# One pool for raw and split weights, a closer second row tile and later transposes in a two-layer decoder trunk

## The chip, the cores and the metric

The kernel runs on one core of one Trainium2 chip. The metric is device time in microseconds (us) of one execution, the median of several runs; lower is better.

## What is computed

The reference is a causal decoder trunk of two layers on 256 rows (two row tiles of 128) with a model width of 2048, all in float32:

```
for layer in range(2):
    u = rms_norm(h, mix_norm_pre[layer])
    u = even_mixer(u, ...) if layer == 0 else odd_mixer(u, ...)
    h = h + rms_norm(u, mix_norm_post[layer])
    u = swiglu(rms_norm(h, ffn_norm_pre[layer]), w_gate, w_up, w_down)
    h = h + rms_norm(u, ffn_norm_post[layer])
```

The even mixer is stick-breaking attention beside a gated DeltaNet, the odd one block-sparse attention beside dilated attention, each between an input and an output projection. `swiglu(u)` is `(silu(u @ w_gate) * (u @ w_up)) @ w_down` with a hidden width of 5632, which is 11 columns of 512. Nearly all the bytes are weights: each is read once and used for both row tiles.

## The kernel before, in words

**Six phases.** `run` (L477) plans six phases and runs them in order with `run_phase`: even in (120 steps), even out (32), FFN of layer 0 (264), odd in (96), odd out (32), FFN of layer 1 (264). A step is one weight piece of 256 rows by 512 columns, 512 KB (some of 16 steps of even in are narrower). `self.load_until` (L224) loads a piece with one DMA on SP's queue into a raw place, splits it into a high and a low part of reduced precision (`split`, L214: ACT's copy at L217, DVE's subtraction at L218) and so makes `w`, 8 KB a partition. `step` (L253) multiplies one row tile with a piece: 2 blocks times 3 products (high by high, high by low, low by high) of 512 columns, L261 to L263. With both row tiles a plain piece is 12 products.

**Fast pieces.** In the FFN most gate and up columns are a `FastChunk` (L80): 5 plain pieces, then 3 fast ones for both row tiles at once with 7 block products in place of 8, each of 3 matmuls of 256 columns (`fast_step`, L270, L285 to L287). A fast piece is 21 matmuls, needs two places for `w`, and four sums of weight blocks on DVE ahead of the split (`split_sums`, L244, L247 to L249). At the chunk's end ACT and DVE put the result together (L291 to L299).

**Places.** There are 3 raw places (`RAW`, a pool of their own) and 10 for `w` (`WB`). The framework hands out the places of a pool in turn, so the DMA of piece k waits for the split of piece k-3, and the split of piece k waits until TensorE is done with what stood in its place ten places ago. The two row tiles are `LAG` = 4 pieces apart (8 at the ends of a phase, `run_phase`, L319); fast pieces bring them together.

**The FFN's order.** `plan_ffn` (L625) takes the 11 columns in groups (0), (1,2), (3,4), ... (9,10). A group's down chunks (4 chunks of 2 pieces a column) stand behind the next group's first gate chunk. So a run of chunks without down chunks between them is up 1, gate 2, up 2, gate 3 (four chunks of 8 pieces), then 16 down pieces, and so on; the last run is up 9, gate 10, up 10, and behind it the down chunks of (9,10) end the phase. An up chunk ends with `up_chunk` (L664): DVE multiplies (L666), then TensorE transposes the product (L364) and ACT and DVE split it for the down products.

**Order and queues.** A scheduler in the framework orders each engine's instructions ahead of time by the order in which they are written and by modelled times; an engine then runs its own strictly in order. SP's queue carries the weight loads and the stores of x to DRAM (`store_x`, L714); POOL's carries the loads of norm weights (L413), the reload of x (L474) and some multiplications (L704). Small working tiles come from a pool of 44 (`mem`), PSUM banks from pools of 5 and 3; in the FFN 3 banks are lent, so that 2 are left for transposes and 6 for sums. Each down chunk's sum is added to y in `down_chunk` (L684), which in the last group also squares it, reloads x and multiplies by the norm weight; `end_ffn` (L708) then puts the norm and the residual together and, in layer 0, stores x.

Of the kernel before, what the change touches and what calls it, by code (L numbers as in the profile page):

```python
# [44 lines left out]
WB = 10  # L45
LAG = 4
# [6 lines left out]
RAW = 3  # L53
# [4 lines left out]
FFN_GROUPS = ((0,), (1, 2), (3, 4), (5, 6), (7, 8), (9, 10))  # L58
# [84 lines left out]
class Builder:  # L143
    def __init__(self, tc, I, out, pool):
        self.tc, self.nc, self.I, self.out = tc, tc.nc, I, out
        self.const = pool("const", bufs=1)
        self.wpool = pool("w", bufs=WB)
        self.rpool = pool("raw", bufs=RAW)
# [4 lines left out]
        self.mem = Pool(big, "m", NTILES)  # L153
        self.ps = Pool(psb, "p", NPS)
# [69 lines left out]
    def load_until(self, n, end=None):  # L224

        nc = self.nc
        while self.loaded < min(n + WB if end is None else end, len(self.steps)):
            s = self.steps[self.loaded]
            if sum(a.places for a in self.steps[n:self.loaded + 1]) > WB:
                break  # L230
            raw = self.rpool.tile([P, 2048], F32, name="raw", tag="raw")
            w = [self.wpool.tile([P, 2048], F32R, name="w", tag="w") for i in range(s.places)]
            if s.pair is None:
                n_ = s.src.shape[2]
                raw = raw[:, :1024].rearrange("p (k n) -> p k n", k=2)[:, :, :n_]
                s.wh, s.wl = (a.rearrange("p (k n) -> p k n", k=2)[:, :, :n_] for a in (w[0][:, :1024], w[0][:, 1024:]))
                nc.sync.dma_start(out=raw, in_=s.src)
                self.split(s.wh, s.wl, raw)
            else:
                nc.sync.dma_start(out=raw[:, :1024], in_=s.src.rearrange("p k n -> p (k n)"))  # L240
                self.split_sums(raw.rearrange("p (b n) -> p b n", b=8), s, *w)
            self.loaded += 1
# [27 lines left out]
    def fast_step(self, s):  # L270
# [17 lines left out]
        if s.last:  # L288
            za, zb, zu = self.now(self.mem, 3)
            u = zu[:, lo]  # L290
# [5 lines left out]
            self.mem.give(zu)  # L296
# [22 lines left out]
    def run_phase(self, lo, hi, end):  # L319

        n0 = n1 = lo
        while n1 < hi:
            edge = n0 - lo < LAG_EDGE or hi - n0 <= LAG_EDGE - LAG
            lag = LAG_EDGE if edge else max(LAG, LAG_EDGE - (n0 - lo - LAG_EDGE) // 2)
            if n0 < hi and self.steps[n0].pair is not None:
                if n0 == n1:
                    self.fast_step(self.steps[n0])
                    n0 += 1
# [9 lines left out]
            else:  # L338
                self.step(1, self.steps[n1])
                n1 += 1  # L340
# [136 lines left out]
    def run(self):  # L477
# [31 lines left out]
        for i, ((lo, hi), end) in enumerate(zip(bounds, ends)):  # L509
            if i % 3 == 2:  # L510
                for j in range(PS_FFN):
                    self.ps.lend(self.pa)
                if i == 2:
                    self.mem.give(*self.lev)
            self.run_phase(lo, hi, end)
            if i % 3 == 2:
# [108 lines left out]
    def plan_ffn(self, layer):  # L625
        chunks, waiting = [], []
        g, u, d = self.I["ffn_w_gate"], self.I["ffn_w_up"], self.I["ffn_w_down"]
        for q, grp in enumerate(FFN_GROUPS):
            down = []
            for c in range(4):  # L630
                pieces = [(d[layer, c, 2 * f + j], (4 * i + 2 * j, 4 * i + 2 * j + 1))
                          for i, f in enumerate(grp) for j in range(2)]
                done = lambda t, acc, c=c, q=q: self.down_chunk(t, layer, q, c, acc)
                down.append(Chunk(pieces, self.lhs_h, done))
            for i, f in enumerate(grp):
# [4 lines left out]
                if i == 0:  # L640
                    chunks += waiting
                if self.fast("ffn_w_up", f):
                    chunks.append(self.col_chunk(u[layer], f, lambda out, i=i, f=f: self.up_fast(i, f, out), FastChunk))
                else:
                    chunks.append(self.col_chunk(u[layer], f, lambda t, acc, i=i: self.up_chunk(t, i, acc)))
            waiting = down
        chunks += waiting
        self.sg, self.hT = [None, None], [[], []]
# [3 lines left out]
    def lhs_h(self, t, kt):  # L652
        return self.operands(self.hT[t], kt)
# [10 lines left out]
    def up_chunk(self, t, i, acc):  # L664
        u = self.sg[t]
        self.nc.vector.tensor_mul(u, acc, u)  # L666
        self.hT[t].append(self.transposed(u))
        self.mem.give(u)

    def up_fast(self, i, f, out):  # L670
# [4 lines left out]
        for t in range(2):  # L675
            self.up_chunk(t, i, out[t])
            self.mem.give(out[t])

    def free_hT(self, t):
        for pair in self.hT[t]:  # L680
            self.mem.give(*pair)
        self.hT[t] = []

    def down_chunk(self, t, layer, q, c, acc):  # L684
        nc = self.nc
        if c == 3:
            self.free_hT(t)
# [26 lines left out]
    def store_x(self, t):  # L714
        for c in range(4):
            self.nc.sync.dma_start(out=self.xd[t * P:(t + 1) * P, c * 512:(c + 1) * 512], in_=self.x[t][c])
# [131 lines left out]
    def softmax_attn(self, t, g):  # L848
# [5 lines left out]
        if self.mask is None:  # L854
            self.mask = self.now(self.mem).rearrange("p (a b) -> p a b", a=2)
            nc.gpsimd.dma_start(out=self.mask, in_=self.I["amask"])
        mask = self.mask[:, g // 2, 2 * P - nk:]
# [453 lines left out]
```

## Time and profile before

| | |
|---|---|
| median of 3 runs | 2465.85 us (2463.9 to 2470.06) |
| the profiled execution: own time, span | 2476.57 us, 2474.8 us |
| TensorE matmul (PE) busy | 2393.2 us, 97% |
| VectorE (DVE) busy | 1725.7 us, 70% |
| ScalarE (ACT) busy | 1205.3 us, 49% |
| GpSimd (POOL) busy | 201.3 us, 8% |
| mean granted TensorE clock | 0.986 of full speed |
| weight loads on SP's queue | 808, 430.10 MB moved on that queue |

The profiled execution is 10.7 us (0.4%) above the median. PE's busy share counts a matmul from its start to a modelled end, and matmuls overlap; how fast TensorE really goes is read from the starts of matmuls and from their count in a stretch. PEld is the loading of the stationary operand. In the views "A <- B" means that A stood idle until B was done.

### The profile page before, as it was taken

The numbers are of one execution on the slowest core, as the hardware profiler recorded it, in microseconds if no ns is written. First come the engines' busy times: TensorE is split into PE (matmuls) and PEld (weight loads), VectorE is DVE, ScalarE is ACT, GpSimd is POOL, SyncE is SP. The second block draws the span as 40 slices with busy tenths as digits, with TensorE's granted clock in tenths as the row PEclk, the third lists the DMA queues.
The fourth block names the chain that finished last, engine by engine and source line by source line (L and its number), as shares of the span: only waits on it lengthen the run. The fifth ranks groups of instructions, "written<-read, shape, count | busy, mean of one in ns | idle before, by whom it ended". The sixth has DMA issues, their size and how long they took to land.

```text
span 2474.8 us, 32450 instructions
## 1 busy us (share of the span) xinstructions
PE 2393.2 (97%) x12235; PEld 1992.8 (81%) x12235; DVE 1725.7 (70%) x2373; ACT 1205.3 (49%) x1537; POOL 201.3 (8%) x241
## 2 busy tenths in 40 slices
PE   9999998999999999999988999999999999999997
PEld 7878877778888878887876888887888888878885
DVE  6655765667787867777767555556778786877775
ACT  6654563554544444544445444454454444444543
POOL 0340361200000000000020000000000000000012
PEclk9999998999999999999998999999999999999998
DMA  7634444364556565656575555565565566465655
GB/s 228 204 131 150 136 141 161 122 210 157 188 186 206 163 211 171 204 170 205 182 260 191 170 170 175 180 227 192 164 187 188 185 184 208 154 215 176 204 189 186
DMA packets 132669, 453.67 MB, mean 183 GB/s; under 512 B 15568, under 2 KB 20944, under 8 KB 132512
## 3 DMA queue, kind: packets, MB, share of 16 engines
q1 hardware_dynamic: 124160, 430.10, 54.3%
q0 software_dynamic: 6192, 20.22, 2.6%
q8 instruction: 96, 1.57, 0.2%
q10 hardware_dynamic: 2160, 1.27, 0.2%
q14 instruction: 61, 0.50, 0.1%
HBM read 443.11 MB, written 8.42 MB: 182 GB/s over the span
## 4 chain that ended last, share of the span: by engine, by line
PE 28%; DMA 24%; DVE 19%; ACT 6%; issue 4%; ACTq 0%; POOL 0%; DVEq 0%; POOLq 0%
DVE w L218 12%; DMA raw<-in_ffn_w_gate 9%; DMA raw<-in_ffn_w_down 8%; DMA raw<-in_ffn_w_up 7%; ACT w L217 6%; PE acc L263 5%; PE acc L261 5%; PE acc L262 5%; PE p L263 3%; PE p L262 3%; PE p L261 3%; DVE m L299 1%; DVE raw L247 1%; DVE raw L248 1%; DVE raw L249 1%
## 5 line engine op out<-in xcount | busy, mean ns | idle before, releaser
L218 DVE TENSOR_TENSOR w<-raw,w 128x1024 fp32r<-128x1024 f32 (+2 forms) x808 | 1085.7, 1350 | 551.8 <-ACT w L217 548.9
L217 ACT ACTIVATE w<-raw 128x1024 fp32r<-128x1024 f32 (+2 forms) x808 | 928.7, 1153 | 993.3 <-DVE raw L249 231.5
L261 PE MATMUL acc<-w,m 128*128 128x512 f32 (+2 forms) x1622 | 643.2, 397 | 14.6 <-ACT w L217 5.6
L262 PE MATMUL acc<-w,m 128*128 128x512 f32 (+2 forms) x1622 | 640.4, 396 | 4.0 <-DVE w L218 3.9
L263 PE MATMUL acc<-w,m 128*128 128x512 f32 (+2 forms) x1622 | 639.9, 396 | 2.0 <-DVE m L218 1.2
L261 PE MATMUL p<-w,m 128*128 128x512 f32 x1106 | 439.8, 399 | 6.8 <-ACT w L217 5.7
L262 PE MATMUL p<-w,m 128*128 128x512 f32 x1106 | 439.3, 397 | 4.0 <-DVE w L218 3.7
L263 PE MATMUL p<-w,m 128*128 128x512 f32 x1106 | 438.5, 397 | 0.2 <-DVE m L218 0.2
L261 PEld LDWEIGHTS acc<-w,m 128*128 128x128 f32 x1622 | 307.6, 190 | 84.2 <-ACT w L217 7.9
L262 PEld LDWEIGHTS acc<-w,m 128*128 128x128 f32 x1622 | 307.5, 190 | 75.2 <-DVE w L218 9.4
L263 PEld LDWEIGHTS acc<-w,m 128*128 128x128 f32 x1622 | 307.5, 190 | 70.6 <-DVE m L218 1.8
L261 PEld LDWEIGHTS p<-w,m 128*128 128x128 f32 x1106 | 208.5, 189 | 56.4 <-ACT w L217 8.2
L262 PEld LDWEIGHTS p<-w,m 128*128 128x128 f32 x1106 | 208.7, 189 | 55.2 <-DVE w L218 8.2
L263 PEld LDWEIGHTS p<-w,m 128*128 128x128 f32 x1106 | 208.5, 188 | 49.6 <-DVE m L218 0.6
L286 PE MATMUL p<-w,m 128*128 128x256 f32 x480 | 133.3, 278 | 0.4 <-DVE w L218 0.4
L285 PE MATMUL p<-w,m 128*128 128x256 f32 x480 | 133.4, 278 | 0.0
L287 PE MATMUL p<-w,m 128*128 128x256 f32 x480 | 133.1, 277 | 0.0
L247 DVE TENSOR_TENSOR raw<-raw 128x512 f32<-128x512 f32 x126 | 86.9, 690 | 49.9 <-DMA raw<-in_ffn_w_up 32.2
L285 PE MATMUL acc<-w,m 128*128 128x256 f32 x402 | 111.9, 278 | 0.0
L286 PE MATMUL acc<-w,m 128*128 128x256 f32 x402 | 111.3, 277 | 0.0
L287 PE MATMUL acc<-w,m 128*128 128x256 f32 x402 | 111.3, 277 | 0.0
L286 PEld LDWEIGHTS p<-w,m 128*128 128x128 f32 x480 | 90.4, 188 | 1.6 <-DVE w L218 1.0
(266 smaller groups left out, 2022.9 us busy)
## 6 DMA issues: line engine op xcount, KB each, us to landing
raw<-in_ffn_w_gate SPq DMA_DIRECT2D x176, 512.0 KB, 4.2
raw<-in_ffn_w_up SPq DMA_DIRECT2D x176, 512.0 KB, 4.3
raw<-in_ffn_w_down SPq DMA_DIRECT2D x176, 512.0 KB, 4.3
raw<-in_ev_w_in SPq DMA_DIRECT2D x104, 512.0 KB, 3.4
raw<-in_od_w_in SPq DMA_DIRECT2D x96, 512.0 KB, 3.5
raw<-in_ev_w_out SPq DMA_DIRECT2D x32, 512.0 KB, 4.3
raw<-in_od_w_out SPq DMA_DIRECT2D x32, 512.0 KB, 4.2
xd<-m SPq DMA_DIRECT2D x24, 256.0 KB, 4.1
```

The source lines that it names most:

```text
L217: self.nc.scalar.activation(h, src, AF.Copy)
L218: self.nc.vector.tensor_sub(l, src, h.bitcast(F32))
L247: nc.vector.tensor_sub(b[:, 4:6], b[:, 0:1].broadcast_to([P, 2, 256]), b[:, 1:3])
L248: nc.vector.tensor_sub(b[:, 6], b[:, 1], b[:, 5])
L249: nc.vector.tensor_sub(b[:, 7], b[:, 3], b[:, 6])
L261: nc.tensor.matmul(acc, xh, s.wh[:, j], start=(s.first and j == 0), stop=False)
L262: nc.tensor.matmul(acc, xh, s.wl[:, j], start=False, stop=False)
L263: nc.tensor.matmul(acc, xl, s.wh[:, j], start=False, stop=end)
L285: nc.tensor.matmul(acc, xh, s.wh[:, b], start=s.first and i in (0, 2), stop=True, **kw)
L286: nc.tensor.matmul(acc, xh, s.wl[:, b], start=False, stop=True, **kw)
L287: nc.tensor.matmul(acc, xl, s.wh[:, b], start=False, stop=True, **kw)
L299: nc.vector.tensor_add(z, z, acc)
```

## The change

Raw and split weights come from one pool of 13 places, handed out first in, first out. A load takes the first free place for raw data and the next one or two for `w`, and gives the raw place back at once (behind the others); `w` places come back when the second row tile has used them. A load is made only while `spare` + (places of the piece) are free: 3 outside the FFN, 5 in it. In the FFN the second row tile is 1 piece behind instead of 4. The FFN's transposes become a generator that lets 5 calls of `advance` (one a step) pass first. The columns are grouped (0,1), (2,3), ... (8,9), (10); the down chunks of (8,9) stand behind up 10, and those of (10) last. The stores of x go to POOL's queue. Two tiles of `mem` are saved. The diff, cut:

```diff
-RAW = 3
+WPLACES = 13
+SPARE = 3
+SPARE_FFN = 5
+LAG_FFN = 1
+DEFER = 5
-FFN_GROUPS = ((0,), (1, 2), (3, 4), (5, 6), (7, 8), (9, 10))
+FFN_GROUPS = ((0, 1), (2, 3), (4, 5), (6, 7), (8, 9), (10,))
...
-            if sum(a.places for a in self.steps[n:self.loaded + 1]) > WB:
+            if len(self.wp.free) < s.places + self.spare:
                 break
-            raw = self.rpool.tile([P, 2048], F32, name="raw", tag="raw")
-            w = [self.wpool.tile([P, 2048], F32R, name="w", tag="w") for i in range(s.places)]
+            place = raw = self.wp.pop(1)
+            s.w = [self.wp.pop(1) for i in range(s.places)]
+            w = [a.bitcast(F32R) for a in s.w]
...
+            self.wp.give(place)
             self.loaded += 1
...
-            za, zb, zu = self.now(self.mem, 3)
-            u = zu[:, lo]
+            za, zb = self.now(self.mem, 2)
+            u = zb[:, lo]
...
-            edge = n0 - lo < LAG_EDGE or hi - n0 <= LAG_EDGE - LAG
-            lag = LAG_EDGE if edge else max(LAG, LAG_EDGE - (n0 - lo - LAG_EDGE) // 2)
+            edge = n0 - lo < LAG_EDGE or hi - n0 <= LAG_EDGE - self.lag
+            lag = LAG_EDGE if edge else max(self.lag, LAG_EDGE - (n0 - lo - LAG_EDGE) // 2)
...
                 self.step(1, self.steps[n1])
+                self.wp.give(*self.steps[n1].w)
                 n1 += 1
                 self.load_until(n1)
...
                 if i == 2:
                     self.mem.give(*self.lev)
+                else:
+                    self.mem.give(self.mask)
+                self.spare, self.lag = SPARE_FFN, LAG_FFN
             self.run_phase(lo, hi, end)
+            self.spare, self.lag = SPARE, LAG
...
-                if i == 0:
+                if f == grp[0] and f != NFC - 1:
                     chunks += waiting
...
+            if f == NFC - 1:
+                chunks += waiting
             waiting = down
...
     def lhs_h(self, t, kt):
+        while kt // 4 not in self.hT[t]:
+            assert self.advance()
         return self.operands(self.hT[t], kt)
...
+    def up_fast(self, f, out):
...
         for t in range(2):
-            self.up_chunk(t, i, out[t])
+            u = self.sg[t]
+            self.nc.vector.tensor_mul(u, out[t], u)
             self.mem.give(out[t])
+            self.work.append(self.up_transpose(t, f, u))
+
+    def up_transpose(self, t, f, u):
+        for i in range(DEFER):
+            yield
+        o = yield from self.ps.take()
+        self.transpose4(o, v4(u))
+        self.mem.give(u)
+        h, l = yield from self.mem.take(2)
+        self.split(h.bitcast(F32R), l.bitcast(F32R), o)
+        self.ps.give(o)
+        self.hT[t][f] = (h, l)
...
     def store_x(self, t):
         for c in range(4):
-            self.nc.sync.dma_start(out=self.xd[t * P:(t + 1) * P, c * 512:(c + 1) * 512], in_=self.x[t][c])
+            self.nc.gpsimd.dma_start(out=self.xd[t * P:(t + 1) * P, c * 512:(c + 1) * 512], in_=self.x[t][c])
```


## Rows read from the trace of the kernel before

**Rows 1.** Windows, six phases: length, PE busy (x), PEld, DVE, ACT, POOL, clock, DMA.
```profile
9.30:431.50 422.20, 402.01 (x2063) 336.08 (x2064) 275.00 (x548) 226.60 (x403) 123.61 (x116) 0.96 0.50 163
431.50:545.60 114.10, 110.47 (x542) 90.18 (x541) 67.70 (x110) 57.89 (x99) 17.24 (x24) 1.00 0.50 160
548.50:1301.90 753.40, 735.52 (x3855) 615.12 (x3855) 572.07 (x704) 360.58 (x369) 23.18 (x32) 1.00 0.60 192
1311.50:1614.50 303.00, 302.27 (x1429) 247.54 (x1430) 167.60 (x209) 142.49 (x206) 9.73 (x19) 0.99 0.55 176
1614.50:1710.20 95.70, 95.70 (x439) 77.65 (x438) 54.43 (x70) 47.19 (x69) 4.97 (x11) 1.00 0.64 210
1713.30:2465.30 752.00, 737.71 (x3855) 618.11 (x3855) 568.40 (x706) 354.95 (x363) 19.89 (x25) 0.99 0.60 188
```

**Rows 2.** Timeline, TensorE at a run's end: start us, us, engine, line, xcount.
```profile
705.79 0.28 PE L285 MATMUL p<-w,m 128*128 128x256 f32 x1
...
706.82 0.39 PE L261 MATMUL acc<-w,m 128*128 128x512 f32 x1
...
709.61 0.40 PE L261 MATMUL acc<-w,m 128*128 128x512 f32 x1
...
718.03 0.66 PE L364 MATMUL p<-ident,m 128*128 128x128 f32 x4 [1.26 <-DVE m L666]
```

**Rows 3.** The chain that ended last, by line, from the page.
```profile
DVE w L218 12%; DMA raw<-in_ffn_w_gate 9%; DMA raw<-in_ffn_w_down 8%; DMA raw<-in_ffn_w_up 7%; ACT w L217 6%; PE acc L263 5%; PE acc L261 5%; PE acc L262 5%; PE p L263 3%; PE p L262 3%; PE p L261 3%; DVE m L299 1%; DVE raw L247 1%; DVE raw L248 1%; DVE raw L249 1%
```

**Rows 4.** Waits of SP's queue: us in total, times, longest us.
```profile
SPq L237 <- DVE w L218: 1316.9, 544, 27.1
...
SPq L716 <- DVE m L446: 22.0, 24, 6.7
```

**Rows 5.** Instructions by line and shape: xcount | busy us, mean ns | idle before.
```profile
L218 DVE TENSOR_TENSOR w<-raw,w 128x1024 fp32r<-128x1024 f32 x666 | 822.6, 1239 | 532.2 <-ACT w L217 530.0
L217 ACT ACTIVATE w<-raw 128x1024 fp32r<-128x1024 f32 x666 | 705.1, 1061 | 726.0 <-DMA raw<-in_ffn_w_down 203.2 <-PE acc L263 178.6 <-DMA raw<-in_ffn_w_gate 114.4
...
L218 DVE TENSOR_TENSOR w<-raw,w 128x1792 fp32r<-128x1792 f32 x126 | 252.7, 2020 | 18.1 <-ACT w L217 17.4
...
L247 DVE TENSOR_TENSOR raw<-raw 128x512 f32<-128x512 f32 x126 | 86.9, 690 | 49.9 <-DMA raw<-in_ffn_w_up 32.2 <-DMA raw<-in_ffn_w_gate 16.7
...
L299 DVE TENSOR_TENSOR m<-m,p 128x512 f32<-128x512 f32 x49 | 33.4, 681 | 0.0
...
L293 DVE TENSOR_TENSOR m<-m,p 128x256 f32<-128x256 f32 x26 | 10.8, 417 | 0.8
```

**Rows 6.** Waits of TensorE, FFN of layer 0.
```profile
PE acc L261 <- ACT w L217: 5.6, 2, 4.8
PE p L364 <- DVE m L666: 5.5, 4, 2.4
```

**Rows 7.** Waits of TensorE, FFN of layer 1.
```profile
PE p L261 <- ACT w L217: 5.7, 1, 5.7
```

**Rows 8.** Busy time at an FFN's entrance and at both FFNs' last down chunks.
```profile
545.00:552.00 7.00, 4.62 (x25) 3.48 (x24) 7.00 (x11) 6.00 (x10) 0.60 (x2) 0.87 0.55 208
1246.00:1270.00 24.00, 17.24 (x72) 12.68 (x72) 13.99 (x18) 10.56 (x12) 5.25 (x10) 0.93 0.86 313
2403.00:2430.00 27.00, 21.18 (x114) 17.69 (x113) 17.20 (x19) 10.64 (x11) 6.40 (x12) 0.87 0.88 300
```

**Rows 9.** Timeline, POOL's loads at the end of the first FFN.
```profile
1245.38 2.13 POOL L474 DMA_DIRECT2D m<-xd  x4
```

**Rows 10.** The chain that ended last: its piece there (start us, us, what).
```profile
1248.34 7.47 DMA raw<-in_ffn_w_down
```

**Rows 11.** Weight loads of L237, even out: from issue to landing.
```profile
DMA to landing us min/median/max: 3.4/4.3/6.9
```

**Rows 12.** Weight loads of L237, odd in: from issue to landing.
```profile
DMA to landing us min/median/max: 3.3/3.5/7.7
```

**Rows 13.** Weight loads of L237, odd out: from issue to landing.
```profile
DMA to landing us min/median/max: 3.4/4.1/5.7
```

More of the change, by code (lines that the diff above doesn't have):

```diff
@@ L146, in __init__ @@
         self.const = pool("const", bufs=1)
-        self.wpool = pool("w", bufs=WB)
-        self.rpool = pool("raw", bufs=RAW)
+        wpool = pool("w", bufs=1)
         self.tmp = pool("tmp", bufs=1)
@@ L153, in __init__ @@
         self.mem = Pool(big, "m", NTILES)
+        self.wp = Pool(wpool, "w", WPLACES, (P, 2048))
+        self.spare, self.lag = SPARE, LAG
         self.ps = Pool(psb, "p", NPS)
@@ L339, in run_phase @@
                 self.step(1, self.steps[n1])
+                self.wp.give(*self.steps[n1].w)
                 n1 += 1
@@ L514, in run @@
                     self.mem.give(*self.lev)
+                else:
+                    self.mem.give(self.mask)
+                self.spare, self.lag = SPARE_FFN, LAG_FFN
             self.run_phase(lo, hi, end)
+            self.spare, self.lag = SPARE, LAG
             if i % 3 == 2:
@@ L630, in plan_ffn @@
             for c in range(4):
-                pieces = [(d[layer, c, 2 * f + j], (4 * i + 2 * j, 4 * i + 2 * j + 1))
-                          for i, f in enumerate(grp) for j in range(2)]
+                pieces = [(d[layer, c, 2 * f + j], (4 * f + 2 * j, 4 * f + 2 * j + 1)) for f in grp for j in range(2)]
                 done = lambda t, acc, c=c, q=q: self.down_chunk(t, layer, q, c, acc)
                 down.append(Chunk(pieces, self.lhs_h, done))
-            for i, f in enumerate(grp):
+            for f in grp:
                 if self.fast("ffn_w_gate", f):
@@ L639, in plan_ffn @@
                     chunks.append(self.col_chunk(g[layer], f, self.gate_chunk))
-                if i == 0:
+                if f == grp[0] and f != NFC - 1:
                     chunks += waiting
[L642 to L645, printed above, removed]
+                chunks.append(self.col_chunk(u[layer], f, lambda out, f=f: self.up_fast(f, out), FastChunk))
+            if f == NFC - 1:
+                chunks += waiting
             waiting = down
         chunks += waiting
-        self.sg, self.hT = [None, None], [[], []]
+        self.sg, self.hT = [None, None], [{}, {}]
         return chunks
     def lhs_h(self, t, kt):
+        while kt // 4 not in self.hT[t]:
+            assert self.advance()
         return self.operands(self.hT[t], kt)
@@ L662, in gate_fast @@
             self.nc.scalar.activation(a, a, AF.Silu)
[L664 to L670, printed above, removed]
+    def up_fast(self, f, out):
         if f == NFC - 1:
@@ L675, in up_fast, with free_hT @@
         for t in range(2):
-            self.up_chunk(t, i, out[t])
+            u = self.sg[t]
+            self.nc.vector.tensor_mul(u, out[t], u)
             self.mem.give(out[t])
[L679 to L682, printed above, removed]
+            self.work.append(self.up_transpose(t, f, u))
[9 more added lines that the diff above has]
+        self.hT[t][f] = (h, l)
+    def free_hT(self, t, q):
+        for f in FFN_GROUPS[q]:
+            self.mem.give(*self.hT[t].pop(f))
     def down_chunk(self, t, layer, q, c, acc):
@@ L686, in down_chunk @@
         if c == 3:
-            self.free_hT(t)
+            self.free_hT(t, q)
         if q == 0:
@@ L854, in softmax_attn @@
         if self.mask is None:
-            self.mask = self.now(self.mem).rearrange("p (a b) -> p a b", a=2)
-            nc.gpsimd.dma_start(out=self.mask, in_=self.I["amask"])
-        mask = self.mask[:, g // 2, 2 * P - nk:]
+            self.mask = self.now(self.mem)
+            nc.gpsimd.dma_start(out=self.mask.rearrange("p (a b) -> p a b", a=2), in_=self.I["amask"])
+        mask = self.mask.rearrange("p (a b) -> p a b", a=2)[:, g // 2, 2 * P - nk:]
         mix, e_, pT = yield from self.mem.take(3)
```

1 line of the change is left out of this document (removed).

## The prediction

> **What bounds the kernel now.** I read the stretches by phase first. PE is busy nearly throughout, but a matmul's busy time overlaps its neighbour's, so I count starts [rows 1]. On the timeline twelve 512-column products start in 709.61 - 706.82 = 2.79 us, 0.2325 each, and nine of 256 columns in 706.82 - 705.79 = 1.03, 0.1144 each [rows 2]; four transposes show 0.66, partly overlapped, and I take 0.11 each. An FFN has 201 plain pieces (2412 products), 63 fast ones (1323) and 120 transposes, which is the 3855 of its row. Without a stall it takes 2412 x 0.2325 + 1323 x 0.1144 + 120 x 0.11 = 560.8 + 151.4 + 13.2 = 725.4 us. The two took 753.4 and 752.0 [rows 1]: **54.6 us are lost in the FFNs**, and no change of order can win more there.
>
> Then the chain that ended last: it runs through loads of the three FFN weights (24%), DVE's subtraction at L218 (12%) and ACT's copy at L217 (6%), and only then through PE [rows 3]. SP's queue tells why. It waited 1316.9 us in 544 loads for L218 [rows 4]: a load leaves when the split of the piece three before it is done, since there are 3 raw places. The stream of weights is a loop of load, copy, subtract, load, with three pieces in it. PE runs dry where this loop is slower than PE.
>
> Where that is: at the end of each run of four fast chunks, PE waits for L218's parts and for the transposes, which wait for L666 behind late splits on DVE [rows 2, 6]; and at the last down chunks, where PE waited 4.8 us at once in layer 0 and 5.7 in layer 1 for L217 [rows 6, 7]. There POOL's burst (x and norm weights [rows 9]) made a weight load take 7.47 us [rows 10] with no piece in reserve. The stretch 1246 to 1270 holds 72 products where 24 / 0.2325 = 103 fit, so about 7.2 us are lost; 2403 to 2430 holds 63 fast and 51 other products, 7.2 + 11.9 = 19.1 of 27 us, so 7.9 [rows 8]. Phase ends: **15 us**. At an entrance 25 products (12 of them transposes) stand in 7 us, 4.3 us of work, 2.7 lost to the norm chain [rows 8]; two of them 5.5. What is left, 54.6 - 15 - 5.5 = **34 us, lies at the run ends**, eight of four chunks and some shorter, about 4 us each.
>
> **The change part by part.**
>
> *One pool, inside the FFN.* I followed the list of free places by hand, in the order in which they come back. With 5 spare, plain pieces still turn over three raw places, and their w places were used ten pieces earlier, as before. In fast chunks it differs: five of eight loads take a place that PE gave back with the piece eight before, so they no longer wait for a split. Such a load can leave one chunk ahead less its own piece: 5 x 12 x 0.2325 + 3 x 21 x 0.1144 = 21.2, less 2.4, 18.8 us before its use. A fast piece needs a landing of 4.1 to 4.3 [rows 11, 13], sums and subtraction of 0.69 + 2 x 0.42 (L248 and L249, taken like the 256-column L293) + 2.02 = 3.55 [rows 5], and a copy of about 1.06 x 1792 / 1024 = 1.86: some 9.6. The loop that bound is open. What is late next is DVE. For a gate and an up chunk it has 10 x 1.239 + 6 x 3.55 of splits, 8 x 0.42 + 4 x 0.68 of putting together and 4 x 0.68 of products and their splits, 12.4 + 21.3 + 3.4 + 2.7 + 2.7 = 42.5 us [rows 5], against PE's 2 x 21.2 + 8 x 0.11 = 43.3. That is 98%: DVE keeps up only if it hardly idles, so a reserve still shrinks through a run, more slowly. Bounds for the 34 us: 0 and 34. I take 20, nearer the gain, since DVE's idle time before plain subtractions is nearly all waits for L217 [rows 5], which an earlier load shortens.
>
> *Lag 1* changes no count of products; with w places ten pieces back it puts the first use some three pieces further from the split. It is part of those 20. *Deferring the transposes* I cost at nothing: they already stand 718.03 - 706.82 = 11 us behind the chunk's last fast product [rows 2], beyond five half-pieces of 6 x 0.2325 = 1.4 us, 7 us; what covers this is L666's delay, and if DVE is early, five half-pieces are still enough. *Two fewer tiles* likewise.
>
> *Groups.* Eleven columns in six groups either way, so products and additions to y stay. The runs become four of four chunks and a last of five (up 8 to up 10) in each FFN, where there were four of four, one of two and one of three. In return 16 down pieces, 16 x 2.79 = 45 us of PE work, stand between up 10 and the first product that needs its transposes. The burst of POOL's loads stays where the tiles of the norm come free, at up 10. Bounds for the 15 us: 0 (the longer run arrives with as little reserve) and 15; I take 10.
>
> *Stores on POOL.* 24 stores leave SP, where they held the queue for 22.0 us in all [rows 4], but at phase ends where weights were not what PE waited for [rows 8], so 0. On POOL each costs an issue of 0.54 (2.13 for four like it [rows 9]); four stand near the power of the norm chain, at worst 2.1 us at each of six norms, 0 as taken, since that power waits for the last store's x anyway.
> The Trainium skill, SBUF — State Buffer, "Who interferes with whom", says that a DMA issued from GpSimd starves while VectorE holds their shared port in a two-port mode, and advises another queue, which speaks against this edit; its section on the bandwidth-pool intuition has an example of 0.62 us growing to 3.1. By that a store would cost 2.5 us more, an estimate, 10 us at a norm whose power stood behind four of them. POOL's four loads took 2.13 us with DVE at work [rows 9], and show no such starving.
>
> *One pool, outside the FFN.* With 3 spare the same list alternates just **two** raw places, and w places come back eleven pieces later. The loop then takes landing + 1.06 + 1.24 + 0.1 for two pieces. Even out: 4.3 + 2.4 = 6.7, 3.35 a piece, against 114.1 / 32 = 3.57 of PE. Odd in: 3.5 + 2.4 = 5.9, 2.95 against 303.0 / 96 = 3.16. Odd out: 4.1 + 2.4 = 6.5, 3.25 against 95.7 / 32 = 2.99 [rows 1, 5, 11 to 13]. Only odd out falls behind, 32 x 0.26 = 8.3 us, under a reserve of 11 - 4 - 1 = 6 pieces, 19 us. Bounds: 0 if ACT and DVE take each piece at once (no gain, since nothing waited there for weights), and 43, rival 1 below. With a quarter of a microsecond of queueing at each of the two, 0.04 x 96 + 0.51 x 32 = 20 us just exceeds the reserve; I take 2.
> The Trainium skill, DMA: Bandwidth & Descriptors, "Anatomy of one DMA", gives 2.0 us + bytes / 436,000 for a DMA (fitted on GpSimd's queue), 3.2 us for 512 KB. By that the loop would take 5.6, 2.8 a piece, and two places would always do, cost 0. The medians here are 3.5 to 4.3 us, so the measurement decides, and the margin is thin.
>
> *Start.* The first seven loads find fresh places and x's loads no longer stand behind waiting weights; then the narrow pieces of even in run on two places. Gain and loss of up to 5 us each; I take -1.
>
> **Sum:** -20 - 10 + 2 - 1 = -29. Against the profiled execution 2476.57 gives 2447.6; its median stands 10.7 lower, so **2437 us**. If everything came in, 54.6 - 5.5 and 5 at the start, 2412.
>
> **The rivals.**
> *(1) Two raw places bind outside the FFN: slower.* Place: L237's loads in odd in and odd out, then even in. If queueing makes the loop 7.2 us, 3.6 a piece, odd in loses 0.44 x 96 = 42, odd out 0.61 x 32 = 20, together 62 less a reserve of 19, 43; even in, at 422.2 / 120 = 3.52, loses 0.08 x 120 = 10, inside its reserve. Then 2466 - 31 + 43 = **2478**. It decides from about 7.0 us (3.5 a piece: 0.34 x 96 + 0.51 x 32 - 19 = 30), where it eats the whole gain. For: DVE is 55% and ACT 47% busy in odd in [rows 1], so a split often finds the engine taken. Against: the loop's parts sum to 5.9 there. Chance 0.17.
> *(2) DVE is the bound at the run ends.* At 98% it lags as before, the transposes wait as before, and the run of five arrives empty: only the start and a little of the ends are won, under 7 us, about **2462**. For: the sum above. Against: in the FFNs DVE was busy 572.07 of 753.4 us [rows 1] and stood waiting for ACT. Chance 0.14.
> *(3) The run ends are won, the phase ends are not,* since the burst meets a reserve used up by five chunks: 2437 + 10 = **2447**. Chance 0.14.
> The forecast has 0.55.
>
> **How the numbers follow.** A measurement of this kernel tells about 0.3%, 7.4 us. Faster by more: the forecast, rival 3 and the lucky edge of rival 2, 0.71; within: the rest of rival 2 and part of rival 1, 0.14; slower: 0.15. The range runs from 2412, all won, to 2474, in which rivals 2 and 3 and the milder part of 1 lie; about 2 in 10 stay outside, nearly all above.
>
> **What would show it.** Right: each FFN at 735 to 742 us between its first and last product; SP's waits for L218 much lower in the FFN, with TensorE as releaser; TensorE's waits at L364 and for L217 at the last down chunks under 2 us each; odd in and odd out within 3 us of 303 and 96. Wrong: ACT's copy at L217 in odd in waiting for loads instead of for PE (rival 1), DVE over 90% busy in a run with L666 still releasing the transposes (rival 2), or a weight load of 7 us behind POOL's burst ahead of a PE wait (rival 3).

## The result and the profile after

The changed kernel takes **2482.6 us** (median of 7 runs, 2476.9 to 2496.1) beside 2465.9 for the kernel before (7 runs): ratio **1.0078, interval 1.0051 to 1.0105**, slower by 0.8%. The forecast was 2437 us, in a range of 2412 to 2474.

The phases, from the first to the last weight product of each, with the gaps between them (us, one profiled execution each, of 2476.6 and 2482.6 us):

| | before | after | difference |
|---|---|---|---|
| even in | 404.8 | 413.2 | +8.4 |
| gap, even out | 17.5, 113.9 | 15.0, 114.2 | -2.2 |
| entrance of the first FFN | 3.0 | 20.9 | +17.9 |
| FFN of layer 0 | 753.3 | 735.0 | -18.3 |
| gap, odd in | 9.7, 303.1 | 10.5, 312.5 | +10.2 |
| odd out | 95.7 | 96.7 | +1.0 |
| entrance of the second FFN | 3.2 | 7.2 | +4.0 |
| FFN of layer 1 | 751.9 | 735.6 | -16.3 |
| tail | 9.6 | 11.6 | +2.0 |

The FFNs win 35 us; everything around them loses 41. (The two profiled executions lie only 6 us apart, since that of before is 10.7 us above its median.) The windows of the changed kernel, which answer to [rows 1], with the two entrances:

```profile
8.50:436.80 428.30, 406.29 (x2066) 336.79 (x2066) 275.21 (x548) 222.42 (x402) 117.66 (x116) 0.96 0.47 159
436.80:550.90 114.10, 110.47 (x538) 89.57 (x537) 56.64 (x88) 49.55 (x84) 15.96 (x20) 1.00 0.40 135
550.90:571.90 21.00, 2.53 (x14) 2.50 (x13) 15.03 (x32) 10.76 (x20) 3.99 (x10) 0.59 0.58 201
571.90:1306.90 735.00, 730.37 (x3857) 616.25 (x3855) 562.56 (x697) 352.94 (x364) 19.59 (x32) 1.00 0.57 196
1317.40:1629.90 312.50, 304.39 (x1430) 248.92 (x1430) 170.06 (x211) 142.48 (x206) 14.18 (x24) 0.98 0.51 174
1629.90:1726.40 96.50, 95.58 (x437) 77.34 (x435) 51.55 (x62) 44.33 (x64) 6.57 (x13) 1.00 0.57 193
1726.40:1733.60 7.20, 3.39 (x17) 3.28 (x16) 5.16 (x11) 3.50 (x11) 0.61 (x2) 0.67 0.61 196
1733.60:2469.20 735.60, 731.39 (x3853) 617.97 (x3851) 563.75 (x706) 351.85 (x364) 20.13 (x29) 1.00 0.56 193
```

Even out is as long as before, 114.1 us, with PE as busy, and yet its DMA share fell from 0.50 to 0.40: whatever went wrong there does not show as a wait of TensorE. It shows behind the phase, in 21 us that hold 14 matmuls. The last 13 loads of even out, and their time to landing:

```profile
L243 SPq DMA_DIRECT2D w<-in_ev_w_out x13: 328/328/328, 506.1 to 541.6; - x13
...
DMA to landing us min/median/max: 3.3/3.4/4.8
```

**The FFN.** The chain by line, of the changed kernel's page, which answers to [rows 3]:

```profile
PE 33%; issue 32%; DMA 14%; DVE 12%; ACT 6%; POOL 3%; ACTq 0%; DVEq 0%; POOLq 0%; SPq 0%
DVE w L223 7%; PE acc L268 5%; PE acc L270 5%; PE acc L269 5%; ACT w L222 5%; PE p L268 4%; PE p L270 4%; PE p L269 4%; DMA w<-in_od_w_in 4%; DMA w<-in_ev_w_in 3%; DMA w<-in_ffn_w_down 2%; DMA w<-in_ffn_w_gate 2%; DMA w<-in_ffn_w_up 1%; DMA w<-in_ev_w_out 1%; POOL m L1062 1%
```

The loads of FFN weights fell from 24% of this chain to 5%, but that overstates the change. "issue" is time in which the engine that the chain stands on waited for nothing that the profile shows. Its longest piece, 641 us from 580.62 us on, lies between two instructions of POOL, so the chain passes nearly the whole first FFN without touching a weight. In the second FFN it runs through weights in both kernels. There, from 1713.3 to 2465.3 us before and from 1733.6 to 2469.2 us after (the view ends each line after 240 characters):

```profile
by line: DVE w L218 16.3%; DMA raw<-in_ffn_w_gate 13.1%; DMA raw<-in_ffn_w_down 10.6%; DMA raw<-in_ffn_w_up 10.5%; ACT w L217 7.8%; PE p L262 5.2%; PE p L263 5.2%; PE p L261 5.2%; issue 4.9%; PE acc L263 3.0%; PE acc L261 2.9%; PE acc L262 
```

```profile
by line: DVE w L223 12.4%; PE acc L270 7.1%; PE p L269 7.0%; PE p L268 7.0%; PE p L270 7.0%; PE acc L269 7.0%; PE acc L268 7.0%; DMA w<-in_ffn_w_down 6.0%; ACT w L222 5.4%; DMA w<-in_ffn_w_up 5.0%; issue 4.5%; DMA w<-in_ffn_w_gate 3.6%; DVE
```

The FFN loads fell from 34% to 15%, and TensorE's products rose. TensorE's waits in the first FFN, which answer to [rows 6], are small:

```profile
PE p L217 <- DVE m L683: 2.7, 6, 1.0
PE acc L293 <- DVE w L223: 1.2, 1, 1.2
PE acc L269 <- DVE w L223: 0.8, 1, 0.8
```

SP's queue waited 310.5 us in this FFN for the subtraction (L223), where it had waited 482.0 before (L218). It now also waits for TensorE's products to give places back, as it never did before. Over the whole run:

```profile
SPq L243 <- PE p L270: 157.9, 57, 5.3
```

**The entrance.** TensorE's longest wait of the whole run is here:

```profile
PE p L372 <- DVE m L467: 18.5, 1, 18.5
```

L467 is the norm's last multiplication. ACT's timeline in this stretch (start us, us, engine, line; in brackets the idle time before and its releaser) shows the chain that ends in it:

```profile
549.04 1.06 ACT L222 ACTIVATE w<-w 128x1024 fp32r<-128x1024 f32 x1 [2.08 <-DMA w<-in_ffn_w_gate]
552.91 1.06 ACT L222 ACTIVATE w<-w 128x1024 fp32r<-128x1024 f32 x1 [2.81 <-DMA w<-in_ffn_w_gate]
554.86 1.06 ACT L222 ACTIVATE w<-w 128x1024 fp32r<-128x1024 f32 x1 [0.90 <-DMA w<-in_ffn_w_gate]
555.83 0.58 ACT L434 ACTIVATE m<-acc 128x512 f32<-128x512 f32 x1
...
556.40 0.59 ACT L434 ACTIVATE m<-acc 128x512 f32<-128x512 f32 x1
...
562.61 0.61 ACT L434 ACTIVATE m<-m 128x512 f32<-128x512 f32 x1
...
565.58 0.61 ACT L434 ACTIVATE m<-m 128x512 f32<-128x512 f32 x1
```

L434 squares the last sums of even out, at 555.83 for the first row tile and 556.40 for the second, side by side, and 5 us behind the later sum (ready at 550.9): splits of FFN weights that waited for their loads stand ahead of it. Before, this line was L426, and it began 1.7 us behind that sum. Its instructions there (duration in ns, first and last start), and L434's after:

```profile
L426 ACT ACTIVATE m<-m x4: 616/618/622, 538.2 to 541.0; 128x512 f32<-128x512 f32 x4
```

```profile
L434 ACT ACTIVATE m<-m x4: 613/613/613, 562.6 to 565.6; 128x512 f32<-128x512 f32 x4
```

These four are the first row tile's second norm. Before, they ran 7 us ahead of the phase's last product (545.6); after, 12 us behind it (550.9). Counting TensorE's products, 48 to each sum, gives the reason: the first tile's last sum was ready at 534.4 and the second's at 545.6 before, at 549.8 and 550.9 after. **The first tile's lead of 11.2 us, under which its norm was hidden, had shrunk to 1.1 us.** As written in the program, the first tile is 8 pieces ahead there, 8 x 6 x 0.2325 = 11.2 us; so it is the scheduler that had moved the second tile's products forward. It orders by modelled times, and the likely reason is that split weights came late in them; that is a reading of the order, which no run shows directly. TensorE waited for no weight in even out, and the first tile's norm chain stood bare behind it.

**Even in.** Between 50 and 240 us ACT waited for loads. Before:

```profile
ACT w L217 <- DMA raw<-in_ev_w_in: 15.3, 12, 2.4
ACT w L217 <- DMA raw<-in_ev_w_abz: 6.7, 6, 1.6
...
ACT w L217 <- DMA raw<-in_ev_w_z: 4.4, 4, 1.4
```

After:

```profile
ACT w L222 <- DMA w<-in_ev_w_in: 67.3, 41, 3.4
ACT w L222 <- DMA w<-in_ev_w_abz: 9.7, 7, 2.9
ACT w L222 <- DMA w<-in_ev_w_z: 7.8, 6, 3.2
```

26.4 us became 84.8. The 16 narrow pieces went out from 44.3 to 72.7 before, 28.4 / 15 = 1.89 us apart, and from 48.4 to 86.3 after, 2.53 apart. Before and after:

```profile
L237 SPq DMA_DIRECT2D raw<-in_ev_w_abz x8: 540/540/653, 44.3 to 58.5; - x8
L237 SPq DMA_DIRECT2D raw<-in_ev_w_z x8: 539/540/562, 60.2 to 72.7; - x8
```

```profile
L243 SPq DMA_DIRECT2D w<-in_ev_w_abz x8: 539/540/651, 48.4 to 66.9; - x8
L243 SPq DMA_DIRECT2D w<-in_ev_w_z x8: 539/540/540, 68.6 to 86.3; - x8
```

### The profile page after: what moved, and what is told of

It is laid out like the page before. It is cut to its first block, busy times and chain, and to the rows that moved or that the text cites. A ratio compares the mean times of both kernels' runs of the same rounds, so it can differ in the third digit from the quotient of the medians.

```text
span 2480.8 us, 32088 instructions
## 1 busy us (share of the span) xinstructions
PE 2391.6 (96%) x12235; PEld 1999.3 (81%) x12235; DVE 1715.6 (69%) x2373; ACT 1190.2 (48%) x1535; POOL 207.6 (8%) x265
## 4 chain that ended last, share of the span: by engine, by line
PE 33%; issue 32%; DMA 14%; DVE 12%; ACT 6%; POOL 3%; ACTq 0%; DVEq 0%; POOLq 0%; SPq 0%
DVE w L223 7%; PE acc L268 5%; PE acc L270 5%; PE acc L269 5%; ACT w L222 5%; PE p L268 4%; PE p L270 4%; PE p L269 4%; DMA w<-in_od_w_in 4%; DMA w<-in_ev_w_in 3%; DMA w<-in_ffn_w_down 2%; DMA w<-in_ffn_w_gate 2%; DMA w<-in_ffn_w_up 1%; DMA w<-in_ev_w_out 1%; POOL m L1062 1%
## 5 line engine op out<-in xcount | busy, mean ns | idle before, releaser
L223 DVE TENSOR_TENSOR w<-w,w 128x1024 fp32r<-128x1024 f32 (+2 forms) x808 | 1083.2, 1353 | 641.1 <-ACT w L222 638.8
L222 ACT ACTIVATE w<-w 128x1024 fp32r<-128x1024 f32 (+2 forms) x808 | 916.8, 1150 | 1066.1 <-DVE w L256 221.1
L268 PE MATMUL acc<-w,m 128*128 128x512 f32 (+2 forms) x1582 | 617.6, 396 | 9.9 <-ACT w L222 4.2
L269 PE MATMUL acc<-w,m 128*128 128x512 f32 (+2 forms) x1582 | 621.6, 394 | 2.4 <-DVE w L223 2.3
L270 PE MATMUL acc<-w,m 128*128 128x512 f32 (+2 forms) x1582 | 621.1, 394 | 0.8 <-DVE m L226 0.6
L268 PE MATMUL p<-w,m 128*128 128x512 f32 x1146 | 456.4, 399 | 0.2 <-ACT m L222 0.2
L269 PE MATMUL p<-w,m 128*128 128x512 f32 x1146 | 455.1, 397 | 0.2 <-DVE w L223 0.2
L270 PE MATMUL p<-w,m 128*128 128x512 f32 x1146 | 455.3, 398 | 0.0
L268 PEld LDWEIGHTS acc<-w,m 128*128 128x128 f32 x1582 | 298.6, 189 | 77.6 <-ACT w L222 5.7
L269 PEld LDWEIGHTS acc<-w,m 128*128 128x128 f32 x1582 | 299.1, 189 | 69.4 <-DVE w L223 5.0
L270 PEld LDWEIGHTS acc<-w,m 128*128 128x128 f32 x1582 | 299.1, 189 | 67.9 <-DVE m L223 1.3
L269 PEld LDWEIGHTS p<-w,m 128*128 128x128 f32 x1146 | 216.3, 189 | 50.0 <-DVE w L223 0.5
L270 PEld LDWEIGHTS p<-w,m 128*128 128x128 f32 x1146 | 216.1, 189 | 50.2
L268 PEld LDWEIGHTS p<-w,m 128*128 128x128 f32 x1146 | 216.5, 189 | 49.3 <-ACT m L222 0.9
L293 PE MATMUL acc<-w,m 128*128 128x256 f32 x462 | 128.2, 278 | 1.6 <-DVE w L223 1.6
L294 PE MATMUL acc<-w,m 128*128 128x256 f32 x462 | 127.9, 277 | 0.0
L292 PE MATMUL acc<-w,m 128*128 128x256 f32 x462 | 127.7, 277 | 0.0
L421 POOL DMA_DIRECT2D m<-in_ffn_norm_post x16 | 8.8, 551 | 1304.4 <-PE p L270 647.5
L293 PE MATMUL p<-w,m 128*128 128x256 f32 x420 | 116.4, 278 | 0.0
L294 PE MATMUL p<-w,m 128*128 128x256 f32 x420 | 116.1, 277 | 0.0
L292 PE MATMUL p<-w,m 128*128 128x256 f32 x420 | 115.6, 278 | 0.0
L254 DVE TENSOR_TENSOR w<-w 128x512 f32<-128x512 f32 x126 | 86.6, 688 | 14.3 <-DMA w<-in_ffn_w_up 13.9
```

Source lines behind the costliest of these rows:

```text
L222: self.nc.scalar.activation(h, src, AF.Copy)
L223: self.nc.vector.tensor_sub(l, src, h.bitcast(F32))
L254: nc.vector.tensor_sub(b[:, 4:6], b[:, 0:1].broadcast_to([P, 2, 256]), b[:, 1:3])
L268: nc.tensor.matmul(acc, xh, s.wh[:, j], start=(s.first and j == 0), stop=False)
L269: nc.tensor.matmul(acc, xh, s.wl[:, j], start=False, stop=False)
L270: nc.tensor.matmul(acc, xl, s.wh[:, j], start=False, stop=end)
```

## The experiments

In these runs the kernel before, timed beside each, took 2475 to 2481 us; so ratios to before count, not times. Three theories: **A**, two raw places outside the FFN; **B**, the stores of x on POOL; **C**, the order in which the scheduler writes splits and norm work.

| run | ratio to before | interval |
|---|---|---|
| after_again | 1.0077 | 1.0056 to 1.0098 |
| three_raw | 0.9926 | 0.9910 to 0.9941 |
| held_raw | 0.9927 | 0.9898 to 0.9955 |
| stores_sp | 1.0082 | 1.0065 to 1.0099 |
| two_raw_on_before | 1.0150 | 1.0130 to 1.0170 |
| three_in_out | 0.9974 | 0.9961 to 0.9987 |
| three_in_in | 1.0020 | 1.0008 to 1.0031 |
| no_lead | 1.0010 | 0.9993 to 1.0027 |
| apart_in_ffn | 1.0005 | 0.9991 to 1.0020 |
| old_groups | 0.9939 | 0.9915 to 0.9962 |
| no_deferral | 0.9937 | 0.9917 to 0.9956 |
| three_raw_sp | 0.9932 | 0.9908 to 0.9955 |
| ffn_lag4 | 0.9893 | 0.9868 to 0.9919 |
| held_lag4 | 0.9881 | 0.9859 to 0.9902 |
| pool_alone | **0.9852** | 0.9830 to 0.9874 |
| pool_groups | 0.9873 | 0.9852 to 0.9893 |
| pool_lag1 | 0.9919 | 0.9903 to 0.9935 |

**after_again** is the change once more.

> The changed kernel as it is, once more beside the other kernels of this call, to see how far its stretches repeat. Theory A (two raw places outside the FFN): ratio 1.008 +- 0.003, the first FFN's entrance 18 to 22 us with TensorE waiting for DVE's line 467, the FFNs 735 to 750 us.

1.0077, entrance 20.5 us, FFNs 737.8 and 743.3: the ratio repeats, and an FFN's length varies by some 8 us between executions.

**three_raw**, undoing the two places:

```diff
-SPARE = 3
+SPARE = 5
```

> The changed kernel with SPARE = 5 in place of 3, so that outside the FFN plain pieces turn over three raw places again (and w places come back ten pieces later, not eleven); a load is then written at most 7 pieces ahead. Theory A (two raw places outside the FFN cost what was lost): 40 us come back, 2482.6 - 40 = about 2443 us, the entrance of the first FFN falls from 21.0 to about 3 us, odd in from 312.5 to about 303. Theory B (the stores of x on POOL's queue hold up the norm chain): no change, 2482 +- 5, entrance still about 20 us. Theory C (what costs is the order in which the scheduler puts splits and norm work on ACT's queue): between, about 2465, since the loads are written later than before the change.

Measured 0.9926, which is 1.52% or 37 us below the change; entrance 5.2 us, even in 402.5, odd in 304.7. Theory A. In even out its loads landed in 4.3 us again (13 of them from 485.8 to 521.2, the last leaving 21.6 us ahead of the phase's end), and the first tile's lead was 542.8 - 531.8 = 11.0 us.

**held_raw**, three places kept for raw data outside the FFN:

```diff
...
-            if len(self.wp.free) < s.places + self.spare:
+            own = self.spare == SPARE
+            if len(self.wp.free) < s.places + (len(self.held) < 3 if own else self.spare):
                 break
-            place = raw = self.wp.pop(1)
+            place = raw = self.held.pop(0) if own and len(self.held) == 3 else self.wp.pop(1)
...
-            self.wp.give(place)
+            if own:
+                self.held.append(self.wp.renew(place))
+            else:
+                self.wp.give(place)
...
+                self.wp.give(*self.held)
+                self.held = []
```

The last two lines give the held places back where an FFN begins.

> The changed kernel with the raw places kept apart outside the FFN: three of the 13 are held and used in turn, ten stay for w, loads are written up to 9 pieces ahead as before the change; in the FFN all 13 are one list as in the change. Theory A: about 2441 us, as three_raw or a little better. Theory B: no change, 2482. Theory C: about 2441 too, but better than three_raw by 15 us or more, since only here are the loads written as far ahead as before.

0.9927, the same as three_raw: writing the loads 9 pieces ahead in place of 7 is worth nothing, so that part of theory C falls.

**stores_sp**, the stores of x back on SP:

```diff
-            self.nc.gpsimd.dma_start(out=self.xd[t * P:(t + 1) * P, c * 512:(c + 1) * 512], in_=self.x[t][c])
+            self.nc.sync.dma_start(out=self.xd[t * P:(t + 1) * P, c * 512:(c + 1) * 512], in_=self.x[t][c])
```

> The changed kernel with the 24 stores of x back on SP's queue, nothing else. Theory A (two raw places): no change, 2483 +- 5, entrance of the first FFN still about 20 us. Theory B (stores on POOL): the 18 us at the first FFN's entrance and 4 at the second's come back, about 2460. Theory C (order on ACT's queue): no change unless the schedule shifts.

1.0082, entrance 21.6 us. Theory B falls. In its profiled execution the FFNs took 749.9 and 750.1 us, longer than in either profiled execution of the change; the ratio shows no difference, and why is open.

**two_raw_on_before**, the suspected cost alone: the kernel before, with two raw places in turn outside the FFN:

```diff
-        self.rpool = pool("raw", bufs=RAW)
+        self.rpool = pool("raw", bufs=1)
...
-            raw = self.rpool.tile([P, 2048], F32, name="raw", tag="raw")
+            r = f"raw{self.loaded % (3 if getattr(self, 'ffn', False) else 2)}"
+            raw = self.rpool.tile([P, 2048], F32, name=r, tag=r)
...
+            self.ffn = i % 3 == 2
             self.run_phase(lo, hi, end)
```

> The kernel before, with only two of its three raw places used outside the FFN (the FFN keeps three, w keeps ten). Theory A: slower by about what the change loses outside the FFN, 2466 + 40 = about 2506 us, with a long wait at the first FFN's entrance. Theory B: no change, 2466 +- 7. Theory C: slower by no more than 10 us, since the loads are written in the old order.

1.0150, 37 us slower: what three_raw gives back. Even in grew from 404.8 to 421.6, the entrances from 3.0 and 3.2 to 7.2 each; the price is the same, but more of it lies in even in, and the long wait at one entrance, which was expected, did not come. There the first tile kept its lead: its second norm (L427) ran from 559.3 us, ahead of the phase's last product at 560.9.

**three_in_out and three_in_in** give the third place back in a part of the phases:

```diff
+            elif i % 3 == 1:
+                self.spare = SPARE_FFN
             self.run_phase(lo, hi, end)
```

(three_in_in has `i % 3 == 0`.)

> The changed kernel with three raw places (spare 5) in even out and odd out alone; even in and odd in keep two. Theory A1 (the two places starve the last pieces of an out phase, and ACT, whose queue holds late splits ahead of the norm's squares, delays the FFN's entrance): 18 us at the first entrance and 4 at the second come back, ratio to before 1.0078 - 22 / 2466 = about 0.999. Theory A2 (the entrance is late because even in already used up the reserve): no more than 5 us come back, ratio about 1.006.

> The changed kernel with three raw places (spare 5) in even in and odd in alone; even out and odd out keep two. Theory A1: the 7.5 us of even in and 9.5 of odd in come back, the first FFN's entrance stays near 20 us, ratio about 1.0078 - 17 / 2466 = 1.001. Theory A2: nearly all comes back, ratio about 0.994, entrance about 3 us.

26 us come back in the out phases (1.0078 - 0.9974), 14 in the in phases. With even in at 403.5 us again, three_in_in kept the long entrance, with even out still on two places and the tiles' last sums ready at 543.6 and 544.8 us; TensorE's wait there:

```profile
PE p L372 <- DVE m L467: 18.0, 1, 18.0
```

In three_in_out it was 1.8 us. So the entrance is made in even out, not by what even in left (A1, not A2).

**no_lead** takes the lead away where weights come in time (three_raw, first tile one piece ahead at the end of the out phases):

```diff
+            if self.together and hi - n0 <= LAG_EDGE:
+                lag = 1
...
+            self.together = i % 3 == 1
             self.run_phase(lo, hi, end)
```

> The kernel three_raw (0.9926) with the first row tile's lead taken away at the end of even out and odd out: in their last 8 pieces the second row tile is one piece behind in place of eight. If the entrance of the changed kernel is long because its first row tile no longer ends 11 us ahead of the second, so that its norm is not covered: the first entrance grows from 5.2 to 15 to 22 us though all weights come in time, the second likewise, ratio about 0.9926 + 30 / 2466 = 1.005. If late splits on ACT's queue are the cause by themselves: entrance 5 to 8 us, ratio 0.993.

1.0010, 0.84% or 21 us slower than three_raw, and the entrances account for it: 18.4 - 5.2 + 11.5 - 3.9 = 20.8. The tiles' last sums were ready at 540.2 and 541.6 us, and TensorE waited for the same line (now L469) at both:

```profile
PE p L374 <- DVE m L469: 15.9, 1, 15.9
...
PE acc L374 <- DVE m L469: 9.1, 1, 9.1
```

So taking away the lead, and nothing else in the program, is enough for a long entrance. In no_lead too the squares (its L436) began late, at 545.5 us, behind splits that waited for FFN loads; what such splits add on ACT was not tried alone.

**Inside the FFN.** apart_in_ffn is held_raw with `own = True` everywhere, three raw and ten other places as before the change; old_groups, no_deferral, three_raw_sp and ffn_lag4 each undo one part on three_raw:

```diff
-FFN_GROUPS = ((0, 1), (2, 3), (4, 5), (6, 7), (8, 9), (10,))
+FFN_GROUPS = ((0,), (1, 2), (3, 4), (5, 6), (7, 8), (9, 10))
...
-            if f == NFC - 1:
+            if f == NFC - 1 and f == grp[0]:
...
-DEFER = 5
+DEFER = 0
...
-            self.nc.gpsimd.dma_start(out=self.xd[t * P:(t + 1) * P, c * 512:(c + 1) * 512], in_=self.x[t][c])
+            self.nc.sync.dma_start(out=self.xd[t * P:(t + 1) * P, c * 512:(c + 1) * 512], in_=self.x[t][c])
...
-LAG_FFN = 1
+LAG_FFN = 4
```

> The kernel held_raw (0.9927) with three raw places and ten for w kept apart in the FFN too, as before the change; lag 1, deferral, groups and stores of the change stay. If one pool gives the 20 us in the FFN that the prediction gave it: ratio 0.9927 + 20 / 2466 = about 1.001, and each FFN about 10 us longer, with TensorE waiting for splits at the run ends again. If the gain is from lag and groups instead: about 0.993 to 0.996.

> The kernel three_raw (0.9926) with the old groups (0), (1,2), ... (9,10). If the groups give the 10 us of the prediction, at the two phase ends: ratio 0.9926 + 10 / 2466 = about 0.997, with TensorE waiting some 5 us for a split at each FFN's last down chunks. If one pool alone already covers the ends: 0.993.

> The kernel three_raw (0.9926) with DEFER = 0, so that the FFN's transposes are written at the end of their up chunk. If deferral costs and gains nothing, as predicted: 0.993. If TensorE, which runs in order, then stands behind the transposes that wait for DVE's product: some 2 us at each of 11 up chunks and each row tile group in 2 FFNs, 22 x 1 to 2 = 22 to 44 us, ratio 1.002 or more.

> The kernel three_raw (0.9926) with the stores of x back on SP's queue. If the stores' queue is worth nothing, as predicted: 0.993. If a store on POOL holds up a norm's power by at most 2 us: 0.991 to 0.993, the tail 9.6 in place of 11.6 us. If stores on SP hold up weight loads at the phase ends: above 0.996, with the FFNs' entrances longer.

> The kernel three_raw (0.9926) with LAG_FFN = 4, the second row tile four pieces behind as before the change. If lag 1 is a part of the 20 us that one pool gave in the FFN, since places come back three pieces earlier: ratio 0.9926 + 10 / 2466 = about 0.997. If one pool gives it by itself: 0.993.

Measured against their base: the pool is worth 0.78%, 19 us; the groups 0.13%, 3 us, within the intervals; deferral and stores nothing, though with the stores on SP the tail is 9.6 us in place of 11.6. ffn_lag4 came out against the expectation: lag 4 is *faster*, by 0.33%, 8 us, though the two intervals still overlap a little. held_lag4, the same edit on held_raw, says so too (0.9881 beside 0.9927, 11 us).

> The kernel held_raw (0.9927) with LAG_FFN = 4. If lag 1 costs 8 us whatever stands outside the FFN: 0.989 to 0.990, the same as ffn_lag4. If ffn_lag4 was faster by the scheduler's order alone: 0.993.

**pool_alone, pool_groups, pool_lag1**: three_raw with all four of these parts undone (the two saved tiles stay), and then with the new groups alone, or with lag 1 alone, put back.

> The kernel before with the one pool of 13 alone: three raw places' worth of spare (5) everywhere, old groups, lag 4, no deferral, stores on SP. If the pool is what gains, and groups (3 us) and lag 1 (a loss of 8 us) add up as in the single runs: ratio 0.9893 + 3 / 2466 = about 0.990. If it needs the new groups or lag: 0.995 or more.

> The kernel pool_alone (0.9852) with the new groups (0,1), ... (10), and nothing else. If the groups are worth something beside the pool, as predicted (10 us) or as old_groups suggests (3 us): 0.981 to 0.984. If the pool already covers the phase ends: 0.985 +- 0.002. If the run of five chunks costs more than the ends give: 0.987 or more.

> The kernel pool_alone (0.9852) with LAG_FFN = 1, and nothing else. If lag 1 costs about 8 us, as between ffn_lag4 and three_raw: 0.988 to 0.989. If it costs only together with the new groups or the deferral: 0.985 +- 0.002.

The pool alone has the lowest ratio, 0.9852, **1.5% faster than before and 2.2% faster than the change**; the intervals of pool_groups and held_lag4 reach into its own. In its profiled execution, the slowest of four, the FFNs took 740.6 and 739.0 us, 25.6 less than before, of the 36.5 that the ratio tells; every other stretch lies within 2 us of before. The groups change nothing that is resolved (0.9873). Lag 1 costs 0.67%, 16.5 us. TensorE's waits for DVE's product ahead of the transposes (L217) and for ACT's split (L222), in the second FFN of pool_lag1, are

```profile
PE acc L217 <- DVE m L683: 6.2, 6, 2.5
PE p L268 <- ACT m L222: 2.8, 1, 2.8
```

and the first of them in pool_alone is

```profile
PE acc L217 <- DVE m L683: 1.0, 1, 1.0
```

That these waits are all of it is not shown; in the two FFNs of the profiled executions the difference was 5.1 + 4.0 = 9.1 us.

## Why the prediction was wrong

- **One pool, inside the FFN (-20): the mechanism right, the number in part luck.** apart_in_ffn gives 19 us, but both kernels compared there have lag 1, which the step had counted into its 20 as a gain. Alone the pool is worth 36 us (pool_alone), and lag 1 takes 16.5 back. What was foretold did show: SP waits less for the subtraction, TensorE releases loads, and FFN loads fell from 34% to 15% of the second FFN's chain. The FFNs took 735.0 and 735.6 us, the near edge of the 735 to 742 forecast (737.8 and 743.3 in after_again).
- **Lag 1 (in those 20): wrong in sign.** That "it puts the first use some three pieces further from the split" holds for the places, but lag 1 costs 8 us on the change's other parts and 16.5 on the pool alone. The step counted products and places and no wait of the transposes; that these waits are the whole cost is not shown.
- **Groups (-10): too large.** 3 us on three_raw, nothing resolved on the pool. The run of five chunks arrives with a reserve, but so does the pool with the old groups: TensorE's longest wait in the second FFN of pool_alone was 1.4 us, so the pool had won the phase ends already.
- **Deferral, two fewer tiles (0): right** for the deferral as far as it is resolved (0.9937 beside 0.9926, inside the intervals); the tiles were not tried.
- **Stores on POOL (0): right** within what can be told. The 24 stores landed in a median 3.6 us from POOL, 4.1 from SP before, and stores_sp changed nothing. The Trainium skill's sentence on starving that was weighed there (SBUF — State Buffer, "Who interferes with whom") speaks of VectorE in a two-port mode, and the same section says that tensor_tensor has none. VectorE's costliest lines here are tensor_tensor (L223 alone 1083.2 of its 1715.6 us), so this trace does not put that sentence to the test. Nor did [rows 9], where VectorE was busy for 0.6 of the 2.3 us. The tail, 11.6 us with the stores on POOL and 9.6 with them on SP, is the one place where they cost; the prediction had allowed 2.1 us at a norm and taken 0.
- **One pool, outside the FFN (2, bounds 0 to 43): this is the step that failed.** It was worth **37 us**. The loop itself came out cheaper than the 3.35 us a piece that the step had for even out; its last 13 loads left from 506.1 to 541.6 us, 35.5 / 12 = 2.96 a piece. Wrong was what it was held against. "114.1 / 32 = 3.57 of PE" is a mean over a phase that begins with the mixers' work; at its end only weight products are left, 12 x 0.2325 = 2.79 a piece. A loop of 2.96 loses against that. And the "reserve of 11 - 4 - 1 = 6 pieces", which the step had for odd out, was not there at the end of even out: ACT split no weight between 477 and 504 us, where before the change seven splits began in that time (486.7 to 502.4). Its longest waits in that hole were 6.2 us for the mixers' products of L860 and 4.3 us for TensorE to free a place. Behind it TensorE kept its pace by using up the first tile's lead, and the bill came at the entrance.
- **Start (-1, bounds 5 each way): failed with it.** Even in was given no pace at all for its narrow pieces; with two places they left 2.53 us apart in place of 1.89, and ACT waited 54 times for loads between 50 and 240 us. 14 us of the loss lie in the in phases, odd in among them, where the step above had found 2.95 us of loop against 3.16 of PE and no loss.
- **The rule on a DMA's time** was set aside because the medians were 3.5 to 4.3 us. With two raw places the loads landed in 3.4 us at the end of even out and 3.2 in even in. So for these stretches the Trainium skill, DMA: Bandwidth & Descriptors, "Anatomy of one DMA" (3.2 us for 512 KB, a fit for GpSimd's queue) agrees with this trace; with three places in even out (4.3) it does not. By it the loop is 2.8, by the runs 2.96. That two places would then "always do" fails all the same, against 2.79.
- **Rival 1** gave 2478 and the time is 2482.6, but by another way: it put the loss into odd in and odd out with a loop of 3.6. The sign that it named did show, ACT waiting for loads (116.2 us in 67 times between 1340 and 1630 us, where before it waited for PE), but odd in lost 9.4 us, all but 1.6 of which came back in three_raw, and odd out 1. The loss lay in even in (8.4), in odd in and, the largest part, at the entrances of the FFNs (17.9 and 4.0), which no rival named: at the first the price of a late first tile is a norm chain, 18 us, not its few late pieces.
- **The whole sum, part by part.** In ratios to before the runs give 0.9852 with the pool alone, 0.9919 with lag 1 added, 0.9926 with groups, deferral and stores too, and 1.0078 with one raw place fewer outside the FFN. In us that is -36.5 + 16.5 + 1.7 + 37.5 = +19, where the forecast had -29. The 1.7 is inside the intervals.

## What to carry to other kernels

Hold a load loop against the pace of the stretch where only weight products are left, not against a phase's mean, and count the reserve as it stands at that point. Where one row tile's lead hides a norm, anything that eats the lead can cost the norm's whole length, and an order that is made ahead of time can hide it: here TensorE waited for no weight until the phase had ended. And a list of places handed out first in, first out, can rotate fewer of them than are spare: follow it by hand, then try one more. Time the parts of a bundle one by one: here one part alone was 2.2% faster than all of them together.

## What was not expected of the hardware

A load's landing was not fixed by its size: 512 KB in even out took a median 4.3 us with three places (before [rows 11], and again in three_raw) and 3.5 with two (3.4 at its end); in odd out it was 4.1 [rows 13] and 3.5. So taking a place away there costs less per piece than 3 to 2 suggests. In odd in it hardly differed, 3.5 [rows 12] and 3.4; what else sets the landing time is not shown.

The granted clock through the first entrance of the changed kernel, and after it (windows, clock third from the end):

```profile
551.00:571.80 20.80, 2.40 (x11) 2.40 (x12) 14.83 (x32) 10.66 (x20) 3.99 (x10) 0.59 0.58 203
571.80:580.00 8.20, 8.20 (x31) 6.37 (x31) 8.13 (x13) 5.79 (x13) 2.20 (x4) 0.80 0.71 245
580.00:600.00 20.00, 20.00 (x102) 16.61 (x101) 14.71 (x29) 8.44 (x13) 0.60 (x2) 1.00 0.32 110
```

While TensorE stood almost idle it fell to 0.59, near the lower of its two levels (1.2 of 2.4 GHz), and it came back late: 0.80 over the first 8.2 us of products, made up of 0.50 up to 575.0 us and 0.99 from there to 580.0. But that is no price of the long entrance. In the kernel before, with an entrance of 3.0 us, the clock was 0.73 over the first 3.5 us of the FFN (548.5 to 552.0) and 0.84 over the next 4.7. So a short idle stretch had cost about as much clock as the long one.
